# Stepping the latent stream's triangular inverses along the context steps of the chunk recurrence

## The chip, the core and the metric

The kernel runs on one core of a Trainium2 chip. The core has a matrix engine (PE, with its weight loads PEld), a vector engine (DVE), an engine for activations and copies (ACT), a general engine (POOL), and SP, which here only issues DMAs. Each engine takes its instructions strictly in order and waits on semaphores for the others. The metric is the device time of one execution in microseconds (us), lower is better; a kernel is told by the median of its runs.

## The reference: what is computed

Two layers act on 256 latent tokens and 256 context tokens of width 1024, all in float32. Layer 0 has two heads groups side by side behind one input projection: a bidirectional RWKV-7 recurrence (8 heads of 64) and a differential attention (4 heads). Layer 1 is a bidirectional Mamba-2 mixer. Each layer ends with a squared-ReLU MLP. The part that matters here is the recurrence of layer 0:

```python
def step(s, inp):
    r_t, w_t, k_t, v_t, kk_t, b_t = inp
    sa = jnp.einsum('bhvk,bhk->bhv', s, -kk_t)
    s = s * w_t[:, :, None, :] + sa[..., None] * b_t[:, :, None, :] + v_t[..., None] * k_t[:, :, None, :]
    return s, jnp.einsum('bhvk,bhk->bhv', s, r_t)
...
yc, sf, sb = wkv_bidir(rc, (s_zero, s_zero))
yl, _, _ = wkv_bidir(rl, (sf, sb))
```

The context runs first, from a zero state, and its two final states (forward and backward) start the latent stream. The attention needs none of this: it reads the same input projection and is joined to the recurrence only by the output projection.

## The kernel before, in words

**The recurrence in chunks.** A stream of 256 tokens is cut in 4 chunks of 64. Within a chunk the recurrence is a triangular system, and the kernel inverts its matrix for every chunk, head and direction ahead of the steps. `R1` and `T1` belong to the context (s = 1), `R0` and `T0` to the latent stream (s = 0).

**The inverses** are made by the generator `rwkv_T` (L443), which is advanced in pieces. Its first piece writes the 64x64 matrices `TT` to DRAM scratch (`Lscr`) and reads the diagonal 32x32 blocks back as `Lp`, and POOL clears `Z`. Then come 31 steps of two DVE instructions each: `tb<-Lp,Z` (L464) and `Z<-Z,tb` (L466). The next piece sends the result on: `Z` to scratch (`Zscr`), ACT makes the transposed copy `Zt` (L90), `Zt` goes to scratch (`Yscr`), and five DMAs bring both back into `TT` and `ZX`. Two last pieces join the 32x32 blocks on PE: 128 small matmuls `wp`, whose result ACT copies to `TT`, and 128 `xp`, copied likewise. `wp` reads what came back from `Zscr`; `xp` reads also what came back from `Yscr`.

**The chunk recurrence** is the generator `rwkv_chain`, called `C`: first 6 pieces that prepare step 0, then 8 steps of 4 pieces, 4 for the context and 4 for the latent stream. A step is a chain over three engines: `rp` on PE, copy `r_` on ACT, `up` on PE (it reads `TT`), copy `UV` on ACT, `sp` on PE, the new state `S` on DVE (two additions and four multiplications), and the next step's `rp` reads `S`. `yp` is its output. Between the pieces `rwkv_pre` prepares the step after: `gp` on PE, masked to `GM` by DVE, and the transposes `tk`, copied to `tok`. The step with number 4 is the first of the latent stream: it needs the last context state and the finished `TT` of `R0`.

**The attention** is the generator `F`: for each of 4 heads the input projection (`inps`, 24 matmuls of 128x512 per third) and four units: scores `sc` on PE, softmax on DVE and ACT into `pt`, transposes `awt`, and `aop`. At the end of a head DVE normalises (`nw_x`, `nw_y`, `nw_t`, nine small instructions), scales `O`, PE transposes it (`aot`), DVE makes `at`, and SP writes it to `mixd` in DRAM, from where the output projection (`wo`) later reads it as `ma`.

**What sets the order.** In this part of the program the generators are advanced in turn by `merge` and `run`: the text below L1043 says which comes when. The order on an engine is not that of the text, though. The compiler of the tile language places each instruction by its place in the text and by when it reckons its operands ready, so an instruction that is ready early can stand before others that the text has ahead of it. What came out is shown below in rows of the order.

**Buffers.** Most of the operands named here (`Lp`, `Z`, `Zt`, `ZX`, `tok`, `GM`) come from one ring of 6 buffers of 4 KB per partition, `r4`. Three accumulator banks (`psc`) are shared by `wp`, `xp`, `rp`, `yp`, `up` and `sp`.

Of the kernel before, what the change touches and what calls it, by code (L numbers as in the profile page):

```python
# [7 lines left out]
F32 = mybir.dt.float32  # L8
# [11 lines left out]
NT = 512  # L20
# [31 lines left out]
def build(ctx: ExitStack, tc, xT, cT, pk_d, ct_d, ca_d, cs_d, lora_d, gup_d, cb_d, ada_w, adaT, w_in, w_out, w1, w2,  # L52
          s_in, s_dt, s_out, out, dbg=None, stop=None):
    nc = tc.nc
    act, dve, pool, pe = nc.scalar, nc.vector, nc.gpsimd, nc.tensor
# [18 lines left out]
    def mm(o, l, r, start=True, stop=True):  # L74
        pe.matmul(o, lhsT=l, rhs=r, start=start, stop=stop)  # L75

    def tt(o, a, b, op):
        dve.tensor_tensor(o, a, b, op)  # L78

    def ts(o, a, s1, op0, s2=None, op1=None):  # L80
        if op1 is None:
            dve.tensor_scalar(o, a, s1, None, op0)
        else:
            dve.tensor_scalar(o, a, s1, s2, op0, op1)
# [4 lines left out]
    def actf(o, i, f, scale=1.0, bias=0.0, **kw):  # L89
        act.activation(out=o, in_=i, func=f, scale=scale, bias=bias, **kw)  # L90
# [4 lines left out]
    def psg(shape, name="g"):  # L95
        return PS["g"].tile(shape, F32, name=name, tag="g")

    def psc(shape, name="ch"):
        return PS["ch"].tile(shape, F32, name=name, tag="ch")
# [156 lines left out]
    def run(*gs):  # L256

        while True:
            for g, n in gs:
                for _ in range(n):  # L260
                    if next(g, g) is g and g is gs[0][0]:
                        return
# [65 lines left out]
    with ExitStack() as c1:  # L328
# [11 lines left out]
        def r4(shape, name):  # L340
            return reg.tile(shape, F32, name=name, tag="r4", bufs=6)
# [90 lines left out]
        def ar_tile(p, name):  # L432
            return p.tile([128, 2, 4, 4, 2, 64], F32, name="AR", tag=name)

        def bk_tile(p, name):
            return p.tile([128, 4, 4, 4, 64], F32, name="BK", tag=name)

        R1, R0 = dict(AR=ar_tile(mid, "ar"), BK=bk_tile(mid, "bk")), {}
# [1 line left out]
            R["PC"] = reg.tile([128, 2, 4, 4], F32, name=f"PC{i}")  # L440
            R["TT"] = reg.tile([128, 4, 8, 64], F32, name=f"TT{i}")

        def rwkv_T(R, s, eng):  # L443

            L_, Z_, Y_ = scr[s]
            TT = R["TT"]
            view = lambda a: a.rearrange("(q m) (r t) -> q r m t", q=4, t=32)
            lv, zv, yv = view(L_), view(Z_), view(Y_)
            m4 = lambda a: a.rearrange("r (c h) t -> r c h t", c=4)
            for d in range(2):  # L450
                for b in range(2):
                    nc.sync.dma_start(out=m4(lv[2 * d + b]), in_=TT[Q(d, b), :, :, 32 * b:32 * b + 32])
            Lp = r4([128, 32, 32], "Lp")
            nc.sync.dma_start(out=Lp, in_=L_.rearrange("p (r t) -> p r t", t=32))
            Z = r4([128, 32, 32], "Z")
            zf = Z.rearrange("p a b -> p (a b)")
            pool.memset(zf, 0.0)
            pool.memset(zf[:, 0:1024:33], 1.0)
            yield
            for q in range(31):  # L460
                n, m = 31 - q, q + 1
                tb = reg.tile([128, 256], F32, name="tb", tag="tb", bufs=1)
                t3 = tb[:, 0:n * m].rearrange("p (a b) -> p a b", b=m)
                eng.tensor_tensor(t3, Lp[:, q, q + 1:32].unsqueeze(2).to_broadcast([128, n, m]),  # L464
                                  Z[:, q, 0:m].unsqueeze(1).to_broadcast([128, n, m]), MUL)
                eng.tensor_tensor(Z[:, q + 1:32, 0:m], Z[:, q + 1:32, 0:m], t3, SUB)  # L466
                yield
            nc.sync.dma_start(out=Z_.rearrange("p (r t) -> p r t", t=32), in_=Z)
            Zt = r4([128, 32, 32], "Zt")
            actf(Zt, Z.rearrange("p a b -> p b a"), AF.Copy)  # L470
            nc.sync.dma_start(out=Y_.rearrange("p (r t) -> p r t", t=32), in_=Zt)
            ZX = r4([128, 4, 8, 32], "ZX")
            for d in (1, 0):
                for b in range(2):
                    nc.sync.dma_start(out=TT[Q(d, b), :, :, 32 * b:32 * b + 32], in_=m4((yv, zv)[d][2 * d + b]))
                nc.sync.dma_start(out=ZX[Q(d, d)], in_=m4((zv, yv)[d][3 * d]))
            tmp = lambda d, c, h: TT[Q(d, 1), c, h, 0:32]
            yield
            for c2 in range(2):
                c_ = slice(2 * c2, 2 * c2 + 2)  # L480
                wp = psc([128, 2, 8, 32], "wp")
                for c in range(2):
                    for h in range(8):
                        cc = 2 * c2 + c
                        mm(wp[Q(0, 1), c, h], TT[Q(0, 0), cc, h, 32:64], ZX[Q(0, 0), cc, h])
                        mm(wp[Q(1, 1), c, h], TT[Q(1, 0), cc, h, 32:64], TT[Q(1, 0), cc, h, 0:32])
                for d in range(2):
                    actf(tmp(d, c_, slice(0, 8)), wp[Q(d, 1)], AF.Copy)
            yield
            for c2 in range(2):  # L490
                c_ = slice(2 * c2, 2 * c2 + 2)
                xp_ = psc([128, 2, 8, 32], "xp")
                for c in range(2):
                    for h in range(8):
                        cc = 2 * c2 + c
                        mm(xp_[Q(0, 0), c, h], tmp(0, cc, h), TT[Q(0, 1), cc, h, 32:64])
                        mm(xp_[Q(1, 1), c, h], ZX[Q(1, 1), cc, h], tmp(1, cc, h))
                actf(TT[Q(0, 0), c_, :, 32:64], xp_[Q(0, 0)], AF.Copy, scale=-1.0)
                actf(TT[Q(1, 1), c_, :, 0:32], xp_[Q(1, 1)], AF.Copy, scale=-1.0)
                pool.memset(TT[Q(0, 1), c_, :, 0:32], 0.0)  # L500
                pool.memset(TT[Q(1, 0), c_, :, 32:64], 0.0)
            yield
# [4 lines left out]
        with tc.tile_pool(name="prep", bufs=1) as pp:  # L507
            def ring(name, shape, bufs):
                return pp.tile(shape, F32, name=name, tag=name, bufs=bufs)
# [172 lines left out]
                        yield  # L682

            krvs, kks, early = [], [], []
            T1, T0 = rwkv_T(R1, 1, dve), rwkv_T(R0, 0, dve)
            after = {}
            step = lambda g, n=1: lambda: [next(g, None) for _ in range(n)]
            for hp in range(4):
# [6 lines left out]
                after.setdefault(28 + hp, []).append(lambda hp=hp: gate(hp))  # L695
            after[26].append(step(T1))
            after[27].append(step(T1, 31))
            after[31].append(step(T0))
            A = ada([(0, m) for m in range(2, 5)], lambda sh, n: ring("arow", sh, 4), 512, 3, (None, nc.scalar)[0])
            with ExitStack():  # L700
                for u, _ in enumerate(units()):
# [9 lines left out]

        at = c1.enter_context(tc.tile_pool(name="at", bufs=1, reuse_waits="tile"))

        S = at.tile([128, 2, 4, 2, 64], F32, name="S")
        pool.memset(S.rearrange("p d h e v -> p (d h e v)"), 0.0)

# [25 lines left out]
        def rwkv_step(R, st, G, s):  # L742
# [4 lines left out]
            ar = lambda d, hp, i: R["AR"][:, d, hp, chs[d], i]  # L747
            sv = lambda d, hp: S[:, d, hp].rearrange("p e v -> p (e v)")
            rp = psc([128, 8, 64], "rp")
# [25 lines left out]
            if st < 3 or s == 1:  # L775
# [5 lines left out]
                for e in range(2):  # L781
                    q = E2[e]
                    Sd = S[q, :, :, e]
                    tt(Sd, sp[q], Sd, ADD)
# [190 lines left out]
        def att_e(hd):  # L975
            O = H[hd][4]
            op = psg([128, NT], "aot")
            for i in range(4):
                pe.transpose(op[:, i * 128:i * 128 + 128], O[:, i // 2, i % 2], ident)
            t1 = ring("at1", [128, NT], 1)  # L980
            ts(t1, op, sub8, MUL)
            nc.sync.dma_start(out=mixd[:, 4 + hd], in_=t1)

# [25 lines left out]
        def merge(main_, fill, share):  # L1009

            b = 0.0
            for _ in main_:
                b += share
                while b > 0:
                    c = next(fill, None)
                    if c is None:
                        break
                    b -= c
# [25 lines left out]
        F = attention()  # L1044
        C = rwkv_chain()
        O1, O0 = chain(rwkv_ln(R1, 1), rwkv_ln(R1, 0), rwkv_out(R1, 1)), rwkv_out(R0, 0)
        with ExitStack():
            merge(islice(F, 18), iter(()), 0)
            next(T1)
            merge(islice(C, 6), F, 1)  # L1050
            run((islice(T0, 32), 1))
            merge(T1, F, 1.5)
            merge(islice(C, 12), F, 3.0)
            while todo or ready:
                next(F)
            merge(islice(C, 4), F, 3.0)
            merge(T0, F, 1)
            merge(islice(C, 4), F, 2.5)
            for _ in F:
                pass  # L1060
# [627 lines left out]
```

## Time and profile before

| | |
|---|---|
| median of 3 runs | 1425.53 us (1421.06 to 1426.71) |
| the profiled execution's own time | 1426.16 us |
| its span, first to last instruction | 1424.4 us |
| busy: PE, DVE, ACT, POOL | 1348.7, 1046.4, 632.3, 264.5 us |
| steps of T1 on DVE | 197.0 to 232.8 us |
| steps of T0 on DVE | 232.8 to 280.1 us |
| last attention matmuls `aop` | end at 376.2 us |
| step 4 of the recurrence | `rp` on the state at 377.9 us, `up` from 382.4 us |

Times in the trace count from the start of the span. A row of the timeline has the start, the duration, the engine, the line, the operation, out<-in by the program's names, the shapes, the count, and in brackets how long the engine had been idle before it and what ended that. A row of the windows has, for a stretch of time, its length and then each engine's busy time with its number of records, the granted PE clock (1.00 is full speed), the share of the DMA engines and GB/s. A float32 matmul leaves up to two records. In the list of groups the busy time and the mean duration stand after the first bar. In the list of DMA issues stand the count, the size and the median time from issue to landing. Lines are those of the kernel before; L75, L78, L82, L87 and L90 are helpers which every matmul, tensor operation and activation goes through, so one goes by the names of the tiles.

### The profile page before, as it was taken

How to read it: one execution, taken by the hardware profiler on the slowest of the kernel's cores; microseconds unless marked ns; L12 is line 12 of the kernel's file. 1: busy time of each engine (PE TensorE's matmuls, PEld its weight loads, DVE VectorE, ACT ScalarE, POOL GpSimd, SP SyncE). 2: the span in 40 equal slices, each digit the busy share in tenths (PEclk: the TensorE clock that was granted, in tenths of full speed). 3: DMA queues.
4: the chain of work that ended last, by engine and by line, in shares of the span. 5: the costliest groups of instructions: out<-in, count | busy, mean ns of one | idle time of the engine just before them, and what ended most of it. 6: DMA issues, size and time to landing. Idle time of an engine off the chain costs nothing.

```text
span 1424.4 us, 25962 instructions
## 1 busy us (share of the span) xinstructions
PE 1348.7 (95%) x10026; PEld 1139.4 (80%) x10026; DVE 1046.4 (73%) x2245; ACT 632.3 (44%) x1186; POOL 264.5 (19%) x196
## 2 busy tenths in 40 slices
PE   6899998999998799999999998999999989999997
PEld 2566666777887788888888997888888879999997
DVE  3788869756778899887666577697778785766665
ACT  2534434444543543223232243765645533555543
POOL 0122342211004200000000001233323335311100
PEclk9999998899999899999999999999999999999998
DMA  9566574134323466666666433754444423566663
GB/s 350 171 187 185 185 200 111 60 77 171 104 85 112 133 201 186 192 191 200 207 195 215 145 103 88 180 146 134 133 119 133 110 84 106 153 186 187 184 185 97
DMA packets 311324, 220.42 MB, mean 155 GB/s; under 512 B 30176, under 2 KB 279840, under 8 KB 310048
## 3 DMA queue, kind: packets, MB, share of 16 engines
q1 hardware_dynamic: 306080, 210.36, 49.8%
q10 hardware_dynamic: 3968, 4.20, 1.0%
q0 software_dynamic: 1152, 4.19, 0.8%
q8 instruction: 79, 1.29, 0.4%
q14 instruction: 45, 0.37, 0.1%
HBM read 205.54 MB, written 13.17 MB: 154 GB/s over the span
## 4 chain that ended last, share of the span: by engine, by line
PE 61%; DVE 5%; ACT 1%; issue 1%; DVEq 0%; ACTq 0%
PE m L75 38%; PE xsp L75 5%; PE zp L75 3%; PE bm L75 3%; PE so L75 3%; PE first L75 1%; PE cm L75 1%; PE ssdy L75 1%; PE hst L75 1%; PE xtp L1434 1%; PE nps L75 0%; DVE cva L87 0%; PE gn L75 0%; PE hlat L75 0%; PE gnb L75 0%
## 5 line engine op out<-in xcount | busy, mean ns | idle before, releaser
L90 ACT ACTIVATE wh<-wraw 128x1024 fp32r<-128x1024 f32 x197 | 208.2, 1058 | 366.4 <-PE m L75 255.6
L75 PE MATMUL m<-hid,wh 128*128 128x256 f32 (+1 forms) x1152 | 256.5, 318 | 0.6 <-DVE hid L78 0.6
L146 POOL TENSOR_TENSOR wl<-wraw,wh 128x1024 fp32r<-128x1024 f32 x55 | 133.2, 2428 | 614.5 <-ACT wh L90 602.5
L146 DVE TENSOR_TENSOR wl<-wraw,wh 128x1024 fp32r<-128x1024 f32 x142 | 173.7, 1223 | 43.8 <-ACT wh L90 43.7
L75 PEld LDWEIGHTS m<-hid,wh 128*128 128x128 f32 x1152 | 190.5, 189 | 17.0 <-DVE hid L78 0.8
L75 PE MATMUL m<-hid,wl 128*128 128x256 f32 (+1 forms) x576 | 183.3, 318 | 0.0
L75 PEld LDWEIGHTS m<-hid,wl 128*128 128x128 f32 x576 | 108.8, 189 | 7.7
L75 PE MATMUL m<-hh,wh 128*128 128x512 f32 (+1 forms) x264 | 103.3, 394 | 0.0
L75 PE MATMUL m<-hh,wl 128*128 128x512 f32 (+1 forms) x264 | 103.1, 393 | 0.0
L75 PE MATMUL m<-hl,wh 128*128 128x512 f32 (+1 forms) x264 | 103.1, 393 | 0.0
L246 DVE CUSTOM_DVE_ANT_0 arow<-arow,cb 128x512 f32<-128x512 f32 x112 | 75.9, 689 | 27.2 <-DMA arow<-in_adaT_dram 26.1
L358 POOL TENSOR_TENSOR rl<-rw,rh 128x512 fp32r<-128x512 f32 x45 | 59.9, 1333 | 187.2 <-ACT rh L90 177.2
L75 PE MATMUL inps<-hh,rh 128*128 128x512 f32 x208 | 90.2, 435 | 2.7 <-ACT hh L90 2.7
L90 ACT ACTIVATE rh<-rw 128x512 fp32r<-128x512 f32 x73 | 45.5, 627 | 95.2 <-PE inps L75 63.1
L75 PE MATMUL inps<-hl,rh 128*128 128x512 f32 x208 | 85.7, 413 | 0.2 <-DVE hl L78 0.2
L75 PE MATMUL inps<-hh,rl 128*128 128x512 f32 x208 | 85.2, 410 | 0.0
L75 PE MATMUL m<-uh,wh 128*128 128x258 f32 x256 | 73.4, 287 | 2.4 <-ACT uh L90 2.4
L75 PE MATMUL m<-ul,wh 128*128 128x258 f32 x256 | 73.3, 286 | 0.0
L75 PE MATMUL m<-uh,wl 128*128 128x258 f32 x256 | 73.2, 286 | 0.0
L75 PEld LDWEIGHTS m<-hh,wh 128*128 128x128 f32 x264 | 50.7, 192 | 11.2
L75 PEld LDWEIGHTS m<-hh,wl 128*128 128x128 f32 x264 | 50.5, 192 | 11.5
L75 PEld LDWEIGHTS m<-hl,wh 128*128 128x128 f32 x264 | 50.5, 192 | 11.1
(690 smaller groups left out, 3340.9 us busy)
## 6 DMA issues: line engine op xcount, KB each, us to landing
wraw<-in_w_dram SPq DMA_DIRECT2D x133, 512.0 KB, 3.9
arow<-in_adaT_dram SPq DMA_DIRECT2D x112, 256.0 KB, 3.3
wraw<-in_s_in_dram SPq DMA_DIRECT2D x48, 512.0 KB, 4.3
rw<-in_w_in_dram SPq DMA_DIRECT2D x52, 256.0 KB, 3.6
arow<-in_ada_w_dram SPq DMA_DIRECT2D x48, 256.0 KB, 3.5
araw<-in_ada_w_dram SPq DMA_DIRECT2D x16, 512.0 KB, 9.3
csb<-csd SPq DMA_DIRECT2D x8, 1024.0 KB, 6.3
wraw<-in_s_out_dram SPq DMA_DIRECT2D x16, 512.0 KB, 3.8
```

What stands on the lines that cost most here:

```text
L75: pe.matmul(o, lhsT=l, rhs=r, start=start, stop=stop)
L90: act.activation(out=o, in_=i, func=f, scale=scale, bias=bias, **kw)
L146: eng.tensor_tensor(l, raw, h.bitcast(F32), SUB)
L246: dve.tensor_tensor_reduce(r if s == ns - 1 else junk, r, cb[:, s, i * W:i * W + W], 0.5, 0.0, MUL, ADD, sums[:, s, j, i:i + 1])
L358: eng.tensor_tensor(l, r, h.bitcast(F32), SUB)
L1434: pe.transpose(tp[:, q, i * 128:i * 128 + 128], xs[:, i, t0:t0 + 128], ident)
```

## The change

```diff
-        def rwkv_T(R, s, eng):
+        def rwkv_T(R, s, eng, tl):
...
-            Lp = r4([128, 32, 32], "Lp")
+            Lp = tl([128, 32, 32], "Lp")
...
-            Z = r4([128, 32, 32], "Z")
+            Z = tl([128, 32, 32], "Z")
...
-            T1, T0 = rwkv_T(R1, 1, dve), rwkv_T(R0, 0, dve)
+            T1 = rwkv_T(R1, 1, dve, r4)
...
-            after[31].append(step(T0))
...
+        T0 = rwkv_T(R0, 0, dve, lambda sh, n: at.tile(sh, F32, name=n, tag=n))
+        next(T0)
...
-            t1 = ring("at1", [128, NT], 1)
+            t1 = r4([128, 2, NT], "at1")[:, 0]
...
-            run((islice(T0, 32), 1))
             merge(T1, F, 1.5)
-            merge(islice(C, 12), F, 3.0)
+            for _ in range(12):
+                merge(islice(C, 1), F, 3.0)
+                run((islice(T0, 3), 1))
             while todo or ready:
                 next(F)
             merge(islice(C, 4), F, 3.0)
             merge(T0, F, 1)
```

In the text, `T0` is now started a little later (behind the preparation stage instead of in its last unit), its `Lp` and `Z` get buffers of their own in the pool `at`, and the head output `at` goes to the ring `r4`. `Zt` and `ZX` stay in `r4`. The 31 steps of `T0`, its way through DRAM and its `wp` and `xp` matmuls, which stood in one piece ahead of the context steps (the matmuls behind context step 3), follow the twelve pieces of the context steps 0 to 2, three at a time. `merge(T0, F, 1)` finds nothing left.

**The vector engine, the end of T0's steps.** The rows have the line, the operation, out<-in and the size. Before:

```order
L464 TENSOR_TENSOR tb<-Lp,Z 128x60
L466 TENSOR_TENSOR Z<-Z,tb 128x2x30
L464 TENSOR_TENSOR tb<-Lp,Z 128x31
L466 TENSOR_TENSOR Z<-Z,tb 128x31
L932 TENSOR_REDUCE st__3106<-sc 128x1
L932 TENSOR_REDUCE st__3111<-sc 128x1
L78 TENSOR_TENSOR GM<-gp,cr 128x512 x2
```

Now:

```order
L464 TENSOR_TENSOR tb<-Lp,Z 128x60
L466 TENSOR_TENSOR Z<-Z,tb 128x2x30
L464 TENSOR_TENSOR tb<-Lp,Z 128x31
L466 TENSOR_TENSOR Z<-Z,tb 128x31
L78 TENSOR_TENSOR GM<-gp,cr 128x512 x2
L933 TENSOR_REDUCE st__3002<-sc 128x1
L933 TENSOR_REDUCE st__3007<-sc 128x1
```

In both programs these are rows 457 to 463 of the engine: T0's first step stands at the same row (330) and its last `Z<-Z,tb` at the same row (460). The rows between differ in neighbours that have changed places.

**The matrix engine, the end of the attention.** `pt` with a number is the softmax of one unit. Before:

```order
L949 MATMUL awt<-ct,pt_3985 128x128 x4
L738 MATMUL tk<-ct,BK 128x128 x4
L75 MATMUL gp<-AR,BK 128x128 x8
L75 MATMUL aop<-vt,awt 128x128 x4
L75 MATMUL rp<-UV,GM 64x64 x2
L75 MATMUL yp<-S,AR 64x128 x3
L75 MATMUL rp<-UV,GM 64x64 x13
L75 MATMUL rp<-S,AR 64x128 x8
L75 MATMUL yp<-S,AR 64x128 x4
L979 MATMUL aot<-ct,O 128x128
```

Now:

```order
L950 MATMUL awt<-ct,pt_3715 128x128 x4
L75 MATMUL sc<-kT,qr 128x256 x2
L75 MATMUL sc<-kT,qT 128x256 x2
L75 MATMUL aop<-vt,awt 128x128 x4
L75 MATMUL gp<-AR,BK 128x128 x7
L75 MATMUL yp<-UV,GM 64x64 x11
L75 MATMUL sp<-UV,tok 64x64 x16
L75 MATMUL yp<-UV,GM 64x64 x4
L950 MATMUL awt<-ct,pt_3810 128x128 x4
L75 MATMUL aop<-vt,awt 128x128 x4
L980 MATMUL aot<-ct,O 128x128 x4
L75 MATMUL gp<-AR,BK 128x128 x8
```

Before, the last `aop` was followed by `rp` and `yp` of step 4, and then by `aot`; the `wp` and `xp` of T0 and all of context step 3 lay before it. Now `aot` stands right behind the last `aop`, the `sp` and `yp` in the piece belong to context step 2, and behind the piece come one `tk` row, `wp` (64 and 64 matmuls), `tk`, 8 `gp`, `tk`, 4 `gp`, `xp`, and only then `rp`, `yp`, `up`, `sp` and `yp` of context step 3.

**The DMA queue of SP and the copies of ACT, T0's way through DRAM.** SP before:

```order
L468 DMA Zscr_419<-Z 128x1024
L471 DMA Yscr_420<-Zt 128x1024
L475 DMA TT_427<-Zscr_419 32x32x32 x2
L476 DMA ZX<-Yscr_420 32x32x32
L475 DMA TT_427<-Yscr_420 32x32x32 x2
L476 DMA ZX<-Zscr_419 32x32x32
L356 DMA rw<-in_w_in_dram 128x4x128
```

SP now, behind the last head's output (`at` with the highest number); `Zscr` and the first two reloads stand further up, among the weight loads (rows 80 to 83 of the queue; the piece starts at row 92):

```order
L983 DMA mixd<-at_3690 128x512
L476 DMA ZX<-Zscr_419 32x32x32
L983 DMA mixd<-at_3915 128x512
L471 DMA Yscr_420<-Zt 128x1024
L1069 DMA x_4419<-in_xT_dram 128x2048
L476 DMA ZX<-Yscr_420 32x32x32
L475 DMA TT_427<-Yscr_420 32x32x32 x2
L1070 DMA x_4420<-in_cT_dram 128x2048
```

ACT now, from the last attention unit's copies on:

```order
L90 ACTIVATE O<-aop 128x128
L90 ACTIVATE junk,ssq<-O 128x128
L90 ACTIVATE Zt<-Z 128x1024
L90 ACTIVATE TT_427<-wp 32x16x32 x4
L90 ACTIVATE tok<-tk 128x512 x3
L90 ACTIVATE TT_427<-xp 32x16x32 x4
L90 ACTIVATE r__4163<-rp 128x512
L90 ACTIVATE mh<-ma 128x512 x2
L90 ACTIVATE UV<-up 64x512 x2
```

The write of `Zt` and the three reloads from it have moved from the input projections to behind the last write of the attention, and one of the two 1 MB loads of `x` stands between the write and the reloads. `r__4163` is the copy of context step 3.

## The prediction

> **What bounds the kernel now.** I read the page first (shares, slices), then the stage of the change by windows, then what ended PE's idle time there, then single rows of DVE and SP.
>
> ```profile
> PE 1348.7 (95%) x10026; PEld 1139.4 (80%) x10026; DVE 1046.4 (73%) x2245; ACT 632.3 (44%) x1186; POOL 264.5 (19%) x196
> ```
>
> PE works 95% of the span, so what a change saves or costs is what it does to PE's idle time, or to the order of what PE waits for. In the stage:
>
> ```profile
> 230.00:240.00 10.00, 8.95 (x45) 7.03 (x42) 9.53 (x29) 6.71 (x15) 3.59 (x3) 1.00 0.70 183
> 240.00:250.00 10.00, 5.74 (x31) 4.46 (x30) 9.59 (x27) 3.31 (x9) 0.66 (x1) 0.90 0.63 103
> 260.00:270.00 10.00, 7.19 (x59) 5.53 (x58) 9.83 (x26) 4.19 (x12) 4.17 (x3) 1.00 0.28 79
> 280.00:290.00 10.00, 10.00 (x202) 8.07 (x197) 0.91 (x3) 7.48 (x13) 3.52 (x4) 1.00 0.64 175
> 290.00:300.00 10.00, 9.89 (x115) 7.81 (x111) 6.95 (x23) 6.53 (x17) 0.80 (x1) 1.00 0.42 66
> 340.00:350.00 10.00, 9.11 (x115) 7.17 (x115) 7.00 (x22) 5.83 (x19) 0.00 (x0) 1.00 0.48 182
> 350.00:360.00 10.00, 8.71 (x144) 7.38 (x143) 8.30 (x34) 4.39 (x13) 0.00 (x0) 1.00 0.15 50
> 360.00:370.00 10.00, 9.92 (x284) 8.65 (x284) 9.20 (x24) 6.12 (x16) 1.03 (x2) 1.00 0.11 35
> 370.00:380.00 10.00, 9.08 (x167) 7.80 (x161) 6.07 (x23) 5.56 (x15) 1.13 (x2) 1.00 0.01 3
> ```
>
> First column behind the stretch is PE's busy time, the third DVE's. From 230 to 270 DVE is full (9.5 to 9.8 of 10) and PE idles; from 280 on PE is full and DVE idles. The inverses cause the first:
>
> ```profile
> L464 DVE TENSOR_TENSOR tb<-Lp,Z x62: 177/378/1753, 197.0 to 279.6; 128x31 f32<-128x31 f32 x4, 128x60 f32<-128x60 f32 x4, 128x87 f32<-128x87 f32 x4, 128x112 f32<-128x112 f32 x4
> PE avp L915 <- DVE st__2476 L82: 4.3, 1, 4.3
> PE wp L75 <- DVE GM L78: 2.0, 1, 2.0
> PE awt L949 <- DVE pt L87: 1.0, 1, 1.0
> PE aot L979 <- DVE O L82: 0.8, 1, 0.8
> 289.14 0.69 DVE L932 TENSOR_REDUCE st__3106<-sc 128x1 f32<-128x512 f32 x1 [9.09 <-PE sc L75]
> ```
>
> The four waits are PE's from 230 to 280, 8.1 us together, all on DVE; behind T0's last step DVE has nothing to do for 9.09 us. So there is something to gain by spreading T0's steps: up to 8.1 us. Behind 290 PE lost 0.11 + 0.89 + 1.29 + 0.08 + 0.92 = 3.3 us in the five windows shown, which is how well attention and recurrence cover each other there.
>
> **The change, part by part.**
>
> *T0's 62 DVE instructions.* The rows of the order say that they do not move: first and last stand at the same rows of DVE, since they were ready early and were placed early whatever the text says. PE's rows up to the context's first `up` are the same too. Value 0. If the spreading were real it would be worth -8.1 (all four waits) and at worst 0, as DVE idles later.
>
> *Buffers of their own; `at` in the ring.* No DVE or PE row before the end of T0 moves for it. Value 0; from -2.0 (the wait of `wp` for `GM`, if it was a ring buffer that held `GM`) to 0.
>
> *`Zt` and its way through DRAM leave the input projections.* That frees 2.1 us of ACT and the SP queue at 282 to 291, where PE is at 10.00 and 9.89. Value 0, at best the 0.11.
>
> *What takes their place.* The attention is now drawn ahead of the recurrence: when its last `aop` ends, only steps 0 to 2 are done, where before step 3 and T0's matmuls were done and step 4 was under way. These remain and have little beside them. Five terms:
>
> (a) The attention's tail with less in between. From a unit's scores to its finished `pt`, and PE's prices for what can stand between:
>
> ```profile
> 367.85 0.69 DVE L932 TENSOR_REDUCE st__3982<-sc 128x1 f32<-128x512 f32 x1 [0.66 <-PE sc L75]
> 371.42 0.75 DVE L87 SCALAR_TENSOR_TENSOR pt<-pt,st__3987,pt 128x512 f32<-128x512 f32 x1
> 375.00 1.16 PE L75 MATMUL aop<-vt,awt 128*128 128x128 f32 x8
> 263.83 1.16 PE L75 MATMUL gp<-AR,BK 64*128 64x128 f32 x16
> 264.92 0.66 PE L738 MATMUL tk<-ct,BK 128*128 128x128 f32 x4
> L75 PE MATMUL up<-r__3936,TT 64*64 64x64 f32 x32 | 1.1, 221 | 0.0
> L78 DVE TENSOR_TENSOR GM<-gp,cr 128x512 f32<-128x512 f32 x5 | 3.4, 687 | 3.3 <-PE gp L75 3.3
> ```
>
> 372.17 - 367.85 = 4.3 us. In the new order the last unit's transposes have in front of them 4 `aop` (1.16), 7 `gp` (1.0), 15 `yp` and 16 `sp` (1.1 each, as `up`): 4.4; but DVE has two `GM` (1.4) in the same stretch, so PE is short by about 1, and by 0.6 more for the copy ahead of `aop`. The unit before it has 2 `aop`, `up`, one `tk`: 2.4 against 4.3, short by 1.9. The one before waits for the normalisation of a head as well, short by 1.7; two earlier ones by some 0.5 each. Sum 6.2. I take 5, since what is late once leaves work for the next gap; ends 2 and 8.
>
> (b) `aot` right behind the last `aop`:
>
> ```profile
> 376.94 0.17 DVE L84 TENSOR_SCALAR nw_x<-ssq 128x4 f32<-128x4 f32 x1 [0.75 <-ACT junk L90]
> 379.13 0.88 DVE L82 TENSOR_SCALAR O<-O,nw_y 128x128 f32<-128x128 f32 x4
> 379.56 0.30 PE L979 MATMUL aot<-ct,O 128*128 128x128 f32 x1
> 380.45 0.75 DVE L82 TENSOR_SCALAR at<-aot,sub 128x512 f32<-128x512 f32 x1 [0.44 <-PE aot L979]
> L78 DVE TENSOR_TENSOR Y<-Y,lnm 128x512 f32<-128x512 f32 x2 | 1.4, 682 | 0.0
> ```
>
> From the end of `aop` (375.00 + 1.16) to `aot` are 3.4 us; before, `rp` and `yp` of step 4 lay in them, now nothing. DVE now has the mean of `Y` (a reduction, a scaling and this subtraction, about 1.5) among the nine small instructions, part of it in their gaps. Value 4.4; ends 3.4 and 4.9.
>
> (c) `xp` waits for the reload of `Zt`:
>
> ```profile
> 284.22 0.34 SPq L471 DMA_DIRECT2D Yscr<-Zt  x1
> 287.05 1.38 SPq L476 DMA_DIRECT2D ZX<-Yscr  x1
> 288.47 1.23 SPq L475 DMA_DIRECT2D TT<-Yscr  x2
> TT<-Yscr SPq DMA_DIRECT2D x2, 128.0 KB, 3.6
> x<-in_xT_dram SPq DMA_DIRECT2D x1, 1024.0 KB, 6.0
> L75 PE MATMUL wp<-TT 32*32 32x32 f32 x64 | 2.2, 191 | 0.0
> ```
>
> From the write of `Yscr` to the landing of the second reload: 289.1 + 3.6 - 284.2 = 8.5 us. The write stands behind the last `at`: 0.75 for `at` and 0.35 for its DMA, so 9.6 us from the end of `aot`. PE has in that time 8 `gp`, `tk`, `wp` (2.2), `tk`, 8 `gp`, `tk`, 4 `gp`: 1.2 + 0.7 + 2.2 + 0.7 + 1.2 + 0.7 + 0.6 = 7.3. Short by 2.3, say 2.5; ends 0 (the copies of `wp` and the banks delay `gp` anyway) and 5 (the 1 MB of `x` in front of the reloads). SP's queue behind holds the second `x` and `ma`, which ACT copies to `mh` between `r_` and `UV` of step 3: hidden if `ma` is there about 8 us after the reloads.
>
> (d) Step 3 alone. From the end of its `rp`:
>
> ```profile
> L90 ACT ACTIVATE UV<-up 64x512 f32<-64x512 f32 x2 | 1.2, 592 | 0.4 <-PE up L75 0.3
> L78 DVE TENSOR_TENSOR S<-sp,S 64x512 f32<-64x512 f32 x4 | 2.7, 684 | 0.1
> L78 DVE TENSOR_TENSOR S<-S,PC 64x256 f32<-64x256 f32 x8 | 3.0, 416 | 0.1
> ```
>
> `r_` 0.6 (half of `UV`'s two), `up` 1.1, `UV` 1.2, `sp` 1.1, `S` 2 x 0.68 + 4 x 0.42 = 3.0: 7.0 us to the next `rp` on `S`. PE has `up`, 4 `gp`, `sp`, `yp` and the first half of the next `rp`: 1.1 + 0.6 + 1.1 + 1.1 + 0.8 = 4.7. Short by 2.3; ends 1 and 3.5.
>
> (e) The 3.3 us of idle time from 290 to 380, which this order replaces: -3.3.
>
> (f) The clock:
>
> ```profile
> 248.00:254.00 6.00, 6.00 (x27) 4.88 (x27) 4.19 (x13) 3.39 (x9) 1.16 (x1) 0.72 0.00 1
> 272.00:280.00 8.00, 8.00 (x118) 6.54 (x116) 6.71 (x26) 4.29 (x9) 1.03 (x2) 0.58 0.08 29
> ```
>
> Behind the wait of 4.3 us the granted clock was 0.72 for 6 us, behind 0.8 and 2.0 close together 0.58 for 8: 6 x 0.28 = 1.7 and 8 x 0.42 = 3.4 us lost. New waits (b) and (c) could bring two such stretches, but small matmuls fill them, and some of the loss falls into waits. I take 1.5; ends 0 and 6.8. The Trainium skill (TensorE: Matmul & The Clock Gate, Part 1) has the gate fall to half speed after an idle window of about 3.4 us. By that, only (b) is long enough, and the term would be at most that window's half, an estimate of 1.7; the second row, where no single wait was over 2.1, speaks against so sharp a limit.
>
> Sum: 5 + 4.4 + 2.5 + 2.3 - 3.3 + 1.5 = **+12.4 us**; with all low ends 2 + 3.4 + 0 + 1 - 3.3 + 0 = +3.1, with all high ends +24.9. Behind step 4 the order of PE is nearly the old one, so I let the delay run through to the end. The profiled execution took 1426.16, so 1438.6; the median is 0.6 lower: **1438 us**.
>
> **The rivals.**
>
> *A, covered.* The waits before 290 to 380 add to 3.3 only; if the new tail is covered as well, (a) is 2, (c) 0 and (d) 1: about +3, 1428.5. For it: DVE and ACT have room there (DVE 6 to 9 of 10). Against: a wait on PE in this order has no other rows to fill it.
>
> *B, heavier.* The reloads queue behind the load of `x`: if `x`, issued 0.4 us behind the write, lands first (6.0), the reloads end at about 0.4 + 6.0 + 3.6 = 10.0 and not 8.5, +1.5; and the clock falls behind (b) and (c) by both prices above, 5.1 in place of 1.5. 12.4 + 1.5 + 3.6 = +17.5, 1443. The Trainium skill (DMA: Bandwidth & Descriptors, Queues, rings and completion order) says that each DMA engine takes descriptors in ring order, which is this queueing; no row before shows a reload behind a large load.
>
> *C, faster.* T0's steps really run later on DVE, beside the context steps, because on the chip `Lp` or `Z` is late or the rows between them wait. Then DVE is free from 233 to 280 and the four waits go: -8.1, and (a) to (f) shrink as step 3 has to come along: 1418. It decides if `tb` ends behind about 290 us in the new trace. Against it: an engine works in order, and T0's steps stand at their old rows.
>
> **How the numbers follow.** Forecast (+5 to +17 by its middle terms) 0.55, A 0.17, B 0.18, C 0.10. The three runs before lie within 0.4%, so 0.5%, 7.1 us, is about what can be told from no change. Slower by more: most of the forecast (0.52), B whole, a little of A (0.02): 0.72. Faster: C, 0.10. Same: the rest of A and the low end of the forecast, 0.18. The range from 1427 to 1447 leaves out C, the lower half of A and the top of B, some 0.2.
>
> **What would show it.** `tb` still ends at about 280 us. PE waits for DVE `O` at `aot` for more than 3 us, near 365 us, and for a DMA at `xp`. The write of `Yscr` comes behind the last `mixd<-at`. Context step 3 runs bare, and `up` of step 4 starts some 8 to 12 us behind its 382.4. From there to the end the two traces run in step. I am wrong if PE idles less than 5 us between 330 and 395, if `tb` has moved, or if the delay at step 4 is made good by the output projection.

## The result, and the profile after

The changed kernel takes 1441.05 us (median of 6, 1437.14 to 1444.23) against 1426.03 us (1421.06 to 1428.62) before: 1.0099 times the time, 95% interval 1.0078 to 1.012. It is slower by 15.0 us, within the predicted range and 3 us above the predicted 1438. The profiled execution took 1440.72 us, with a span of 1439.0 us.

T0's steps have not moved. The two tiles of the inverse, in the answer for one tile (count, shortest/median/longest duration in ns, first and last start of T1's and T0's steps together):

```profile
L464 DVE TENSOR_TENSOR tb<-Lp,Z x62: 179/377/1753, 198.1 to 281.4; 128x31 f32<-128x31 f32 x4, 128x60 f32<-128x60 f32 x4, 128x87 f32<-128x87 f32 x4, 128x112 f32<-128x112 f32 x4
```

The last of them starts at 281.4 us, against 279.6 before. So nothing that the spreading of the steps could bring can be seen here, and the loss lies elsewhere. Where it lies is read from windows by stage. Before (columns: stretch, length, busy time of PE, PE's weight loads, DVE, ACT, POOL, each with its records; granted clock; DMA share; GB/s):

```profile
200.00:285.00 85.00, 74.34 (x583) 57.24 (x583) 74.39 (x223) 37.91 (x87) 23.08 (x21) 0.90 0.43 110
285.00:340.00 55.00, 54.83 (x645) 43.70 (x640) 29.50 (x84) 25.95 (x65) 9.13 (x7) 1.00 0.43 122
340.00:400.00 60.00, 55.95 (x1017) 47.54 (x1018) 46.27 (x148) 32.16 (x78) 2.16 (x4) 1.00 0.34 116
400.00:480.00 80.00, 68.94 (x663) 59.64 (x663) 65.25 (x144) 33.26 (x68) 23.76 (x18) 1.00 0.39 119
```

After:

```profile
200.00:285.00 85.00, 74.29 (x576) 57.32 (x575) 75.58 (x224) 36.36 (x87) 23.87 (x22) 0.90 0.42 109
285.00:340.00 55.00, 55.00 (x559) 43.89 (x558) 30.42 (x91) 26.95 (x69) 8.92 (x7) 1.00 0.36 119
340.00:400.00 60.00, 49.94 (x778) 41.65 (x778) 30.24 (x95) 24.16 (x57) 2.07 (x4) 0.77 0.38 112
400.00:480.00 80.00, 76.52 (x906) 64.95 (x906) 64.33 (x152) 33.60 (x64) 17.52 (x14) 1.00 0.28 86
```

Up to 340 us the two traces agree. From 340 to 400 PE's idle time has grown from 4.0 to 10.1 us and the mean clock has fallen from 1.00 to 0.77. In windows of 1 us, the sum of PE's busy time times what is missing from the full clock is 11.9 us, and nothing before. I use these two numbers, idle time and loss by the clock, for every run below. Together the stage costs 18.0 us more. From 400 to 480 PE idles 7.6 us less than before: a part is made good in the output projection. Over the whole span, which is 14.6 us longer, PE's idle time has grown by 5.3 us (75.7 to 81.0) and the loss by the clock by 8.5 us (30.0 to 38.5).

What PE waited for from 290 to 400 (engine, tile and line, releaser: total, times, longest), the longest three:

```profile
PE aot L980 <- DVE O L82: 4.8, 2, 4.5
PE gp L75 <- ACT tok L90: 2.1, 2, 1.4
PE yp L75 <- ACT UV L90: 1.1, 1, 1.1
```

There is no wait for a DMA. T0's way through DRAM, on the queue of SP:

```profile
348.44 0.32 SPq L983 DMA_DIRECT2D mixd<-at  x1
363.02 0.32 SPq L476 DMA_DIRECT2D ZX<-Zscr  x1
372.06 0.32 SPq L983 DMA_DIRECT2D mixd<-at  x1
372.47 0.38 SPq L471 DMA_DIRECT2D Yscr<-Zt  x1
375.64 0.32 SPq L476 DMA_DIRECT2D ZX<-Yscr  x1
376.01 2.78 SPq L475 DMA_DIRECT2D TT<-Yscr  x2
```

Before, the write of `Zt` and the reloads stood between 284 and 291 us. T0's inverse is done at 281.8 us (280.1 before); the first load of `ZX` is issued 81 us later, and `Zt` is written out 91 us later. What SP waited for at that first load, from 285 to 395 us:

```profile
SPq L476 <- PE yp L75: 14.2, 1, 14.2
```

`yp` of context step 2 reads `GM`, a tile of the ring: the load of `ZX` stood until its buffer was free. The copy that makes `Zt` did not wait on ACT; it stands in ACT's order behind the last copies of the attention (366.3 us), and its write then stands on SP behind the last `mixd<-at`. One more thing can be read from these times: the load for `wp` landed at 366.5 us, inside the wait at `aot` (365.7 to 370.1 us). By its operands `wp` could have filled the rest of that wait, but in PE's order it stands behind `aot`.

And the clock (windows of 2 and 4 us):

```profile
366.00:368.00 2.00, 0.00 (x0) 0.00 (x0) 2.00 (x7) 1.99 (x3) 0.00 (x0) 1.00 0.04 14
368.00:370.00 2.00, 0.00 (x0) 0.00 (x0) 1.72 (x11) 0.27 (x1) 0.00 (x0) 0.66 0.00 0
374.00:378.00 4.00, 4.00 (x131) 3.71 (x130) 1.29 (x2) 1.28 (x3) 0.60 (x2) 0.50 0.99 330
378.00:382.00 4.00, 2.63 (x20) 2.23 (x19) 0.00 (x0) 2.16 (x4) 0.44 (x1) 0.50 0.89 135
386.00:390.00 4.00, 4.00 (x137) 3.87 (x137) 0.24 (x1) 1.42 (x3) 0.71 (x2) 0.50 0.08 30
392.00:394.00 2.00, 2.00 (x34) 1.83 (x34) 0.00 (x0) 0.60 (x1) 0.00 (x0) 0.87 0.03 8
```

The clock drops in the long wait at `aot` and stays at half for some 24 us, in which PE is busy most of the time, with matmuls that take up to twice theirs.

### The profile page after: what moved, and what is told of

It reads as the page before. It is cut to its first block, busy times and chain, and to the rows that moved or that the text cites. A ratio compares the mean times of both kernels' runs of the same rounds, so it can differ in the third digit from the quotient of the medians.

```text
span 1439.0 us, 25966 instructions
## 1 busy us (share of the span) xinstructions
PE 1358.0 (94%) x10026; PEld 1146.0 (80%) x10026; DVE 1046.9 (73%) x2245; ACT 632.6 (44%) x1186; POOL 264.6 (18%) x196
## 4 chain that ended last, share of the span: by engine, by line
PE 59%; DVE 5%; ACT 1%; issue 1%; DVEq 0%; ACTq 0%
PE m L75 37%; PE xsp L75 5%; PE zp L75 3%; PE bm L75 3%; PE so L75 2%; PE first L75 1%; PE cm L75 1%; PE ssdy L75 1%; PE hst L75 1%; PE xtp L1436 1%; DVE cva L87 0%; PE gn L75 0%; ACT wh L90 0%; PE gnb L75 0%; PE hlat L75 0%
## 5 line engine op out<-in xcount | busy, mean ns | idle before, releaser
L75 PEld LDWEIGHTS m<-hl,wh 128*128 128x128 f32 x264 | 50.1, 190 | 11.1
```

## The experiments

Each kernel ran beside the kernel before on the same chip. The table has the medians with the intervals of the ratio, and, from each profiled execution, PE's idle time + loss by the clock in four stretches. Behind 400 us the kernels are at different points of the program, so the last column says less than the others.

| kernel | median us | ratio, 95% | 200-285 | 285-340 | 340-400 | 400-480 |
|---|---|---|---|---|---|---|
| before | 1426.03 | 1 | 10.7+8.4 | 0.2+0 | 4.0+0 | 11.1+0 |
| the change | 1441.05 | 1.0078-1.012 | 10.7+8.5 | 0+0 | 10.1+11.9 | 3.5+0 |
| x1_debt | 1439.64 | 1.0082-1.0118 | 10.7+8.2 | 0.3+0 | 8.1+9.4 | 8.0+0 |
| x2_reset | 1432.10 | 1.0025-1.0053 | 10.6+8.1 | 0.4+0 | 8.4+5.8 | 5.8+1.7 |
| x6_busy | 1438.28 | 1.0069-1.01 | 12.2+8.5 | 0+0 | 6.4+4.8 | 5.0+5.1 |
| x3_own | 1427.22 | 0.999-1.0022 | 12.3+8.9 | 0+0 | 4.2+0 | 7.6+0 |
| x7_debt_own | 1429.83 | 1.0004-1.0048 | 12.2+8.6 | 0.3+0 | 7.1+0.2 | 5.2+9.7 |
| x12_zt | 1439.58 | 1.0055-1.0108 | 12.3+8.5 | 0+0 | 8.8+8.2 | 4.7+0 |
| x5_gate | 1423.11 | 0.996-0.9986 | 4.0+1.7 | 4.1+0 | 8.0+1.7 | 10.7+2.7 |
| x5b_gate_own | 1429.72 | 1.0008-1.0043 | 3.1+1.7 | 5.6+1.7 | 6.8+8.5 | 7.6+0 |
| x8_gate_t1 | 1422.80 | 0.9969-1.0003 | 5.3+2.7 | 1.5+0.7 | 6.6+0 | 11.8+2.3 |
| x10_own_gate | 1425.81 | 0.9967-1.0005 | 6.3+1.7 | 4.5+3.4 | 4.6+1.7 | 7.4+0 |
| x14_gate_dve | 1423.52 | 0.996-0.9994 | 5.3+3.1 | 3.7+2.0 | 4.7+0 | 11.6+0.4 |
| x15_debt_gate_dve | 1420.94 | 0.9954-0.9995 | | | | |

The profiled executions of x7_debt_own (1437.75 us) and x15_debt_gate_dve (1434.07 us) lie 8 and 13 us above the medians of their kernels, so the first is read with care and the second is left out. Those of x8_gate_t1, x10_own_gate and x14_gate_dve lie 3 to 4 us below theirs.

**Is it the loop's form?** `merge` keeps a budget: each piece of the recurrence adds 3.0 to it, and units of the attention are drawn until it is used up, so that a unit of 2.5 too much is a debt against the next piece. The change calls `merge` once for each piece, and each call begins at zero. That draws the attention ahead, which is what the prediction built on. Two runs: the change with the debt kept, and the kernel before with only the loop cut up.

```diff
-            for _ in range(12):
-                merge(islice(C, 1), F, 3.0)
-                run((islice(T0, 3), 1))
+            def pieces():
+                for _ in islice(C, 12):
+                    yield
+                    run((islice(T0, 3), 1))
+            merge(pieces(), F, 3.0)
```

> The change with one merge over its twelve pieces in place of twelve merges, so that what a piece has drawn too much from the attention is kept as a debt against the next one; T0's three steps per piece stay inside. Theory (the loop's form draws the attention ahead, and that alone costs the time): step 3 of the recurrence is back beside the attention, the 4.5 us wait of aot on O shrinks under 1 us, the clock stays above 0.8 from 360 to 390, and the time is the one before, 1426 +-4. Rival (own buffers, or T0's two matmul groups drawn out of the input projections, cost it): it stays at 1436 to 1441, with the same order of attention and recurrence as before.

The other, against the kernel before:

```diff
-            merge(islice(C, 12), F, 3.0)
+            for _ in range(12):
+                merge(islice(C, 1), F, 3.0)
```

> The kernel before with only the loop's form changed: twelve merges of one piece each, every one starting at a budget of zero; buffers, T0's place in the text and its way through DRAM as before. Theory (the reset alone costs the time): slower than before by 8 to 17 us, 1434 to 1443, with aot right behind the last aop or step 3 bare. Rival (the spread of T0 and its buffers cost it): 1426 +-4.

Measured: 1439.64 and 1432.10 us. My theory fell with the first: the recurrence is back beside the attention and the time is not back. The rival's time came, though not its order. What PE waited for longest from 285 to 400 in that run, then SP's rows of T0:

```profile
PE wp L75 <- DMA ZX<-Zscr: 3.9, 1, 3.9
```

```profile
351.45 0.32 SPq L471 DMA_DIRECT2D Yscr<-Zt  x1
351.86 0.38 SPq L476 DMA_DIRECT2D ZX<-Zscr  x1
354.65 0.32 SPq L476 DMA_DIRECT2D ZX<-Yscr  x1
```

T0's inverse is done at 282.8 us here, so its tiles are 69 us late too, and now PE waits for them itself. The second run says that the reset alone does cost something where T0 stands as before: some 6 us, less than the 8 to 17 expected. Its place is not the one expected either: the last `aot` waits 0.2 us. Its longest wait from 285 to 400 is this:

```profile
PE xp L75 <- issue: 3.2, 1, 3.2
```

The trace names no releaser for it, and the half clock follows until 391.7 us. That wait and that half clock are 7.3 of the 14.2 us lost from 340 to 400; what holds `xp` there stays open.

**Is it the wait at `aot`, by the clock?** Matmuls whose result is overwritten fill the wait; the rest of PE's order from 340 to 400 stays as it is.

```diff
             op = psg([128, NT], "aot")
+            if hd == 3:
+                wl, vl = H["last"]
+                for i in range(28):
+                    mm(op[:, i % 4 * 128:i % 4 * 128 + 128], wl[:, i % 4], vl[:, i % 4], True, True)
```

> The change with 28 extra 128x128 matmuls between the last aop and the last aot, which write into aot's own tile and are overwritten by its transposes; they wait for nothing that the last aop did not wait for, and PE's order is otherwise the same row for row. They take 28 x 0.145 = 4.1 us of a wait that was 4.46 us. Theory (that wait drops TensorE's clock, which then stays at 0.50 for some 20 us): the granted clock from 370 to 390 stays at 0.9 or more, gp x16 takes 1.16 in place of 2.08 us and wp x64 2.2 in place of 3.6, and the time falls by 6 to 9 us, to 1432 to 1435. Rival (the wait itself is the loss, the low clock falls into waits that are there anyway): no change, 1441 +-3, or slower by the part of the 4.1 us that does not fit.

Measured: 1438.28 us, 2.8 us less than the change, with intervals that overlap: inconclusive. Rows of PE, and windows behind them:

```profile
364.67 6.42 PE L75 MATMUL aot<-vt,awt 128*128 128x128 f32 x56
370.92 0.60 PE L985 MATMUL aot<-ct,O 128*128 128x128 f32 x4
371.45 1.16 PE L75 MATMUL gp<-AR,BK 64*128 64x128 f32 x16
```

```profile
376.00:378.00 2.00, 0.04 (x2) 0.04 (x2) 0.00 (x0) 1.86 (x4) 0.00 (x0) 1.00 1.00 352
380.00:384.00 4.00, 3.31 (x48) 2.77 (x48) 0.00 (x0) 0.60 (x1) 0.00 (x0) 0.50 0.69 168
420.00:424.00 4.00, 4.00 (x25) 2.88 (x26) 2.58 (x6) 1.61 (x3) 0.00 (x0) 0.50 0.51 149
```

The filler was too long: I had taken 0.145 us for each matmul from a row that counts two records for each, and it took 6.42 and not 4.1 us. Behind it the `gp` run at 1.16 us, as before, where they took 2.08 in the change; but the next wait (2.0 us, `gp` for `tok`, 376 to 378) brings the half clock, and a wait of 1.43 us at 418 brings it once more. The loss by the clock from 340 to 480 is 9.9 us, against 11.9 in the change: most of it is moved, not taken away.

**Is it the ring?** `Zt` and `ZX` are asked for from the ring of six, in the text now behind the tiles of the context steps, so each gets its buffer when an earlier tile is done with it. Here they take the buffers of `Lp` and `Z`, which are free when T0's steps are done; the loop is that of the change.

```diff
-            Zt = r4([128, 32, 32], "Zt")
+            Zt = tl([128, 32, 32], "Lp")
...
-            ZX = r4([128, 4, 8, 32], "ZX")
+            ZX = tl([128, 4, 8, 32], "Z")
```

> The change as it is, with Zt and ZX in the buffers of Lp and Z. In PE's order the first 19 to 51 matmuls of wp then stand ahead of the last awt and aop, and the last aot behind a part of step 3's rp, in place of right behind aop. Theory (wait and half clock go together, and both come from what stands bare): the 4.5 us wait of aot falls under 1.5 us, the loss by the clock from 340 to 400 from 11.9 to under 6 us, and the time from 1441 to 1429 to 1435. Rival (the tail stays bare since the attention is drawn ahead): 1437 to 1442.

Measured: 1427.22 us, no difference from before that can be told (0.999 to 1.0022), and better than I had expected. SP's rows (the tiles now go by `Lp` and `Z`), and the stage:

```profile
287.00 0.34 SPq L471 DMA_DIRECT2D Yscr<-Lp  x1
291.33 0.50 SPq L476 DMA_DIRECT2D Z<-Yscr  x1
294.13 0.74 SPq L476 DMA_DIRECT2D Z<-Zscr  x1
```

```profile
340.00:400.00 60.00, 55.83 (x1051) 45.97 (x1050) 44.39 (x138) 29.78 (x70) 2.07 (x4) 1.00 0.34 112
```

T0 is back from DRAM before 300 us. With that the order is another: `wp` stands from 362.6 on between the last `awt` and `aop` of the attention, in place of behind `aot`, and `aot` stands in the middle of `rp`. The longest wait at `aot` is 0.5 us, and the clock stays at 1.00 from 285 to 480. The attention is still drawn ahead; it costs nothing that can be seen, since T0's 256 small matmuls are there to fill its tail.

Two more runs check this. The same two lines in the run with the debt kept:

> The run with the debt kept (1439.6 us), and T0's last two tiles, Zt and ZX, no longer take slots of the shared ring of six buffers but the buffers of Lp and Z, which are free by then. There wp waited 3.85 us for the load of ZX, which stood behind a ring slot, and the clock was at half speed for most of 355 to 380: PE lost 8.1 us idle and 9.4 us by the clock from 340 to 400, against 4.0 and 0 before. Theory (the late ring slot is the wait, and the wait brings the half clock): the wait of wp is gone, the loss by the clock from 340 to 400 falls below 3 us, and the time falls to 1425 to 1431. Rival (small matmuls with little beside them hold the clock down whoever waits): the wait goes but the clock is low all the same, 1434 to 1439.

Measured: 1429.83 us, 9.8 us less than without the two lines; the loss from 340 to 400 has gone from 8.1+9.4 to 7.1+0.2. (The 9.7 us of clock loss behind 400 in its profiled execution may be what puts that execution 8 us above the median.) The four runs with and without the two lines, and with and without the debt, thus agree: 1441.05 and 1439.64 us with both tiles in the ring, 1427.22 and 1429.83 us with both out of it. And only the first of the two lines in the change:

> The change with only Zt in a buffer of its own (Lp's); ZX stays in the shared ring of six. Theory (each ring tile that is asked for between the context steps is late by itself, and the last of the two holds T0's matmuls): PE's order keeps aot right behind the last aop and step 3 behind all of T0's matmuls, the loss from 340 to 400 by idle time and clock stays above 14 us, and the time stays at 1435 to 1442. Rival (the write of Yscr behind the last mixd<-at, so Zt alone, was the delay): 1426 to 1431.

Measured: 1439.58 us. The write of `Yscr` is early, but `ZX` holds all of it up:

```profile
286.62 0.34 SPq L471 DMA_DIRECT2D Yscr<-Lp  x1
362.56 0.32 SPq L476 DMA_DIRECT2D ZX<-Yscr  x1
371.99 0.42 SPq L476 DMA_DIRECT2D ZX<-Zscr  x1
```

So the early write of `Yscr` gains nothing: `ZX` alone, late in the ring, keeps the whole loss. `wp` reads the part of `ZX` that comes from `Zscr`, and the load of that part now stands behind the last `mixd<-at` (371.61 us). PE's order has `aot` right behind the last `aop` again, and the wait there is 4.46 us as in the change. The opposite run, with `Zt` alone in the ring, was not made, so what `Zt` costs by itself is not shown.

**What is T0's spreading worth where it really happens?** T0's steps do not move since they are ready early. In this run they cannot be: the first element of `Z`, which is 1, is made from the recurrence's state S after step 0, as S x 0 + 1. The debt is kept, and T0's pieces follow from the fifth on, four at a time.

```diff
+            if gate is not None:
+                ts(zf[:, 0:1], gate(), 0.0, MUL, 1.0, ADD)
...
-        T0 = rwkv_T(R0, 0, dve, lambda sh, n: at.tile(sh, F32, name=n, tag=n))
+        T0 = rwkv_T(R0, 0, dve, lambda sh, n: at.tile(sh, F32, name=n, tag=n), lambda: S[:, 0, 0, 0, 0:1])
```

> As the first of these runs (debt kept), and T0's first element is multiplied out of the recurrence's state S, so that T0's steps really cannot begin on DVE before step 0 has written S; four steps per piece from the fifth piece on. Theory (the four waits of PE for DVE from 230 to 280, 8.1 us, come from T0's steps on DVE): tb begins behind 290, those waits fall to under 2 us, and the time falls to 1418 to 1424. Rival (T0's steps then hold up the attention's tail on DVE from 330 to 390, or T0's matmuls wait at the end for the late inverse, and the gain is given back): 1425 to 1435.

Measured: 1423.11 us, ratio 0.996 to 0.9986: faster by 0.27%. The stages:

```profile
200.00:285.00 85.00, 80.94 (x721) 62.80 (x720) 62.96 (x181) 44.26 (x108) 24.62 (x22) 0.98 0.42 108
285.00:340.00 55.00, 50.87 (x593) 40.54 (x593) 49.69 (x147) 22.38 (x57) 7.83 (x6) 1.00 0.39 119
340.00:400.00 60.00, 52.04 (x951) 43.94 (x946) 43.36 (x136) 29.48 (x66) 2.07 (x4) 0.97 0.42 129
```

Up to 285 us PE loses 5.7 us in place of 19.1: more than the 8.1 us of the four waits, since 8.4 of the 19.1 were the clock. Behind it DVE has 20 us more to do from 285 to 340 (49.7 against 29.5), and 9.6 of the 13.4 us are given back by 400. The same with `Zt` and `ZX` out of the ring:

> The run gated by S (1423.1 us) with Zt and ZX in the buffers of Lp and Z. Its largest waits are on DVE (awt for pt 3.6 us, aot for O 2.0), and none on the loads of T0. Theory (DVE, which has T0's steps beside the attention's tail, sets its end): no change, 1421 to 1425. Rival (ring slots are what holds T0's last part): 1416 to 1420.

Measured: 1429.72 us, where no change was expected. The row of ACT for T0's copy, and PE's largest wait from 285 to 400:

```profile
328.76 1.96 ACT L90 ACTIVATE Lp<-Z 128x1024 f32<-128x1024 f32 x1 [3.61 <-DVE Z L468]
```

```profile
PE sc L75 <- ACT O L90: 2.8, 1, 2.8
```

With a buffer at hand, the transposing copy stands early in ACT's order, at a time at which DVE has not finished: ACT stood 3.6 us, and `O<-aop` behind it, for which PE waited. The late ring slot had kept that copy out of ACT's way. This is only the smaller part of the difference, though. From 285 to 340 the run loses 7.3 us, 3.2 more than x5_gate; from 340 to 400 it loses 15.3 us, 5.6 more, of which 8.5 are half clock from 361.7 to 375.4 us. What brought that is not shown.

**Starting T0 earlier.** Gated by T1's finished inverse in place of S (T0's steps then begin at 268.0 and 270.5 us), once with the debt kept and once as in the change, both out of the ring:

```diff
-        T0 = rwkv_T(R0, 0, dve, lambda sh, n: at.tile(sh, F32, name=n, tag=n), lambda: S[:, 0, 0, 0, 0:1])
+        T0 = rwkv_T(R0, 0, dve, lambda sh, n: at.tile(sh, F32, name=n, tag=n), lambda: R1["TT"][:, 0, 0, 32:33])
```

> As that run, and T0's first element is multiplied out of T1's finished inverse, so that T0's steps on DVE begin when T1's matmuls are done (about 265 us) and run through DVE's empty stretch from 265 to 320, in place of 230 to 280 (before) or 300 to 350 (the run gated by S, 1423.1 us). Theory: from 200 to 285 PE loses 6 us by idle time and clock in place of 19, as with the gate by S (10.7 + 8.4 before, 4.0 + 1.7 there), and the attention's tail from 300 on is not held up by T0 (there 8.0 us idle from 340 to 400, and 4.1 from 285 to 340): 1412 to 1419. Rival (what is gained ahead of 285 is given back behind it all the same, since DVE's work has only moved): 1422 to 1428.

> The change with Zt and ZX in buffers of their own (1427.2 us), and T0's first element multiplied out of T1's finished inverse, so that T0's steps on DVE begin at about 265 us. PE's order is that of the ungated run, row for row; only DVE's order differs. Theory (T0's steps on DVE are what PE waits for between 230 and 280, and cost 8.1 us of waits and 6 us by the clock): from 200 to 285 PE loses 6 to 9 us in place of 21.2, behind it the loss grows by no more than 4, and the time falls by 9 to 13 us, to 1414 to 1418. Rival (most of what is gained there comes back as waits behind 285, as in the two gated runs so far, which gained 13 us ahead of 285 and only 3 in the time): 1421 to 1425.

Measured: 1422.80 and 1425.81 us, both at or near the rival's numbers. In the second PE's order is that of x3_own but for three records, and DVE's differs, so it is the cleanest price: the loss up to 285 falls from 21.2 to 8.0 us, and 7.9 us come back from 285 to 340, behind one wait. ACT:

```profile
313.38 1.97 ACT L90 ACTIVATE Lp<-Z 128x1024 f32<-128x1024 f32 x1 [5.16 <-DVE Z L468]
315.25 0.26 ACT L90 ACTIVATE O<-aop 128x128 f32<-128x128 f32 x1
```

and PE:

```profile
PE sc L75 <- ACT O L90: 4.5, 1, 4.5
```

It is the same copy. So in the last two runs DVE makes it, right behind its own last step:

```diff
+            if gate is not None:
+                ts(Zt, Z.rearrange("p a b -> p b a"), 1.0, MUL)
+            else:
                 actf(Zt, Z.rearrange("p a b -> p b a"), AF.Copy)
```

> The run gated by T1's inverse with the attention ahead (1425.8 us), and T0's transposing copy Zt<-Z is done by DVE right behind its last step, in place of ACT. There ACT stood 5.16 us at that copy until DVE had ended T0's steps (313.4 us), the copy itself took 2.0, and PE waited 4.53 us for the ACT copy O<-aop behind it, with the clock at 0.83 from 310 to 320: 7.9 us lost from 285 to 340, where the ungated run lost nothing. Theory (the copy, standing at the head of ACT, gives back the gain): from 285 to 340 PE loses under 3 us, and the time falls by 3 to 7 us, to 1419 to 1423. Rival (DVE itself, with its extra copy of 1 to 2 us, holds up the attention at the same place): 1424 to 1428.

> The same exchange in the run with the debt kept and T0 gated by T1's inverse (1422.8 us). There ACT stood only 1.22 us at the copy and PE lost 2.2 us from 285 to 340. Theory: little to gain, 0 to 2 us, 1420.5 to 1423. Rival (DVE's extra copy holds up the attention): 1424 to 1427.

Measured: 1423.52 and 1420.94 us (0.996 to 0.9994 and 0.9954 to 0.9995 of before), some 2 us below the runs without, but the intervals overlap: a gain is not shown. The first had expected 3 to 7 us and a loss under 3 us from 285 to 340; that loss is 5.7 us, so its theory holds in part at most. On DVE the copy is twice as fast as on ACT:

```profile
308.85 1.03 DVE L82 TENSOR_SCALAR Lp<-Z 128x1024 f32<-128x1024 f32 x1
```

```profile
PE rope L75 <- DVE at L82: 3.3, 1, 3.3
```

but PE still waits 3.3 us, two groups of matmuls further on, now for DVE: a theory of the copy alone explains 2.2 of the 7.9 us. The lowest median, 1420.94, is 0.3% below the kernel before (0.9974); x5_gate comes to the same (0.9973) with the narrower interval. That is near the limit of what can be told, the more so as it is the best of several versions, and two of its twelve executions took 1432.44 and 1434.07 us.

## Why the prediction was right, and where it was not

The sign, the size and the place (340 to 395 us) were right. The cause that it gave was not, and the sum came out by luck, from errors that cancel: the waits were 4.8 us too high, the clock 10.4 too low, and 3.0 of the stage's 18.0 us do not appear in the time.

- *T0's 62 instructions do not move, value 0.* Right: the last starts at 281.4 us, and PE's loss from 200 to 285 is the same 19.1 us. The most that real spreading could bring, -8.1, left out the clock behind those waits: the gated runs gain 11 to 14 us there. It also left out that DVE's work only moves, so that the times of these runs lie between 5 us under and 4 us above that of before.
- *`Zt` and its way through DRAM leave the input projections, value 0.* This is the step that failed. I asked what their going would free. Of their coming late I priced only `xp`'s wait for the reload, in (c), and not that T0's matmuls are then missing from the attention's tail; that they stayed in the ring was in the front of the document. With two buffers the time goes from 1441.05 to 1427.22 us.
- *The attention is drawn ahead, and therefore the tail is bare.* Not as a cause by itself: x3_own draws it ahead just so, and PE idles 4.2 us from 340 to 400, against 4.0 before. Only with T0's matmuls missing from it is the tail bare. In the kernel before, where these stand behind step 3 in the text, the drawing ahead costs some 6 us, and of what that run loses from 340 to 400, half stands at T0's own `xp`.
- *(a) the tail, 5.* PE idles 3.6 us from 340 to 366, a little less. *(b) `aot`, 4.4.* Measured 4.5; right. *(c) `xp` for the reload, 2.5.* No such wait: at half clock `wp` took 3.6 and `gp` twice their time, and the reload was there first (its last part landed at 382.4 us, `xp` began at 386.1). In its place PE waited 2.1 us at `gp` for `tok`. *(d) step 3 alone, 2.3.* The chain took the 6.9 us expected (7.0) from the end of its `rp`, but PE waited only 0.25 us in it: `yp`, `gp`, the `rp` on `GM` of step 4 and `tk` filled the rest. *(e) -3.3* was right. The waits came to +6.1 in place of +10.9.
- *(f) the clock, 1.5, at most 6.8.* The worst size: 11.9 us. I had built it from two stretches of 6 and 8 us in the trace before; here one lasted 24.
- *The delay runs through to the end.* Wrong: 7.6 us less idle time from 400 to 480, of which some is lost again behind it. `up` of step 4 came 19.8 us behind its old time and not 8 to 12; the time is 15.0 us longer.
- *The rivals.* A (covered) did not occur, though x3_own is what it would have looked like. Its sum was off as well: 12.4 less 3.0, 2.5 and 1.3 is +5.6, and +3 comes out only with (b) and (f) at their low ends. B had the heavier clock right, if not its size (5.1 against 11.9 us). Its queue came true too: the reloads ended 9.9 us behind the issue of the write (10.0 in B), but no wait of PE hung on them. C did not occur, by the sign that was named for it.

What stays open: how the 18 us divide between the waits and the clock, had either come alone. The one run that kept PE busy moved the half clock to the next wait. Open, too, is what `Zt` alone in the ring costs.

## What to carry to other kernels

A step that is moved in the text takes its place in a shared ring of buffers along: ask for each of its tiles which tiles now stand in front of it in the ring, for one that is late holds everything behind it, and the filler work with it. An early buffer is no gift either, if it puts an instruction that still waits at the head of an engine's queue. And price a new wait on the matrix engine with its clock: here the half clock behind the waits cost more than the waits.

## What was not expected of the hardware

The clock has, in windows of 2 us, only the values 1.00 and 0.50 besides windows in which it changes. In all fourteen traces its changes lie whole multiples of 3.41 us apart, and the half clock lasts from 3.4 us at a time to the 23.9 us of the changed kernel. PE's being busy did not bring it back soon. From x1_debt, in which PE waited 1.15 us at 365.9:

```profile
366.00:368.00 2.00, 0.98 (x8) 0.96 (x8) 1.72 (x7) 1.45 (x4) 0.00 (x0) 1.00 0.00 0
368.00:372.00 4.00, 4.00 (x112) 3.67 (x112) 1.53 (x4) 1.53 (x5) 0.52 (x1) 0.53 0.02 4
372.00:376.00 4.00, 4.00 (x76) 3.82 (x72) 0.00 (x0) 1.51 (x3) 0.52 (x1) 0.50 0.02 4
376.00:378.00 2.00, 2.00 (x22) 1.89 (x18) 0.00 (x0) 0.60 (x1) 0.00 (x0) 0.50 0.00 0
```

PE is fully busy for 10 us and stays at half clock for all but the first instants of them. These are small matmuls: `xp`, 32x32, and `rp`, 64x64. In the kernel before a wait of 2.7 us between large ones left the clock alone:

```profile
428.00:431.00 3.00, 0.29 (x2) 0.32 (x3) 3.00 (x5) 0.81 (x2) 1.96 (x2) 1.00 0.32 84
431.00:435.00 4.00, 4.00 (x24) 3.43 (x23) 3.69 (x11) 1.25 (x3) 1.30 (x1) 1.00 0.35 105
```

The Trainium skill (TensorE: Matmul & The Clock Gate, Part 1) has the clock return after one busy window of about 3.4 us. The rows above, with 10 us, do not agree. That small matmuls count for less than large ones in whatever is measured would fit these rows, and so would the place of a wait within the steps of 3.41 us; no run here tested either.

The spread between executions of one kernel goes with this clock: of the twelve of x15_debt_gate_dve the fastest took 1415.77 us at a mean granted clock of 0.982 and the slowest 1434.07 us at 0.968.
